# Spreading the modulation products of a two-block transformer kernel over its stages anew

## The chip, the cores and the metric

The kernel runs on one core of a Trainium2 chip. The core has four engines that compute (PE for matmuls, VectorE written DVE, ScalarE written ACT, GpSimd written POOL) and SyncE (SP), which here issues most of the transfers. The metric is the time of one execution on the device in microseconds, less is better; it is the median of three runs.

## The reference, cut to what matters

Two blocks are applied in turn to x, 256 tokens of 2048 features. The first block has two layers (differential attention, then forgetting attention with shared keys and values), the second has one layer (an S5 state-space mixer with a GLU, then an MLP). Every layer's shift, scale and gate come from a product of a conditioning vector with a large matrix; these are the modulation products.

```python
def first_block(x, c, w_mod, ...):
    c_act = jax.nn.silu(c)
    for l in range(2):
        shift, scale, gate = jnp.split(c_act @ w_mod[l] + b_mod[l], 3, axis=-1)   # 2048 x 6144
        h = x * (1.0 + scale[:, None]) + shift[:, None]
        if l == 0:
            y = diff_attention(h, a_w_in, a_w_out, ...)
        else:
            kshift, kscale = jnp.split(c_act @ kv_w_mod + kv_b_mod, 2, axis=-1)   # 2048 x 4096
            k, v, F = project(x * (1.0 + kscale[:, None]) + kshift[:, None], kv_w)
            y = forgetting_attention(h, b_w_in, b_w_out, k, v, F)
        x = layer_norm(DN_ALPHA * x + gate[:, None] * y, ln_g[l], ln_b[l])
    return x

def second_block(x, c, ctx, c_ctx, w_mod, ...):
    sh1, sc1, gt1, sh2, sc2, gt2 = adaln(c, w_mod)           # silu(c) @ w_mod + b: 2048 x 12288
    csh1, csc1, *_ = adaln(c_ctx, w_mod)
    h_lat = modulate(rmsnorm(x, norm_mix_pre), sh1, sc1)
    h_ctx = modulate(rmsnorm(ctx, norm_mix_pre), csh1, csc1)
    # a complex linear recurrence over the tokens in both directions, then gelu and GLU
    y = s5_mixer(h_ctx, h_lat, ...)
    x = x + gt1 * rmsnorm(y, norm_mix_post)
    h = modulate(rmsnorm(x, norm_mlp_pre), sh2, sc2)
    return x + gt2 * rmsnorm(jnp.square(jax.nn.relu(h @ w_mlp_in)) @ w_mlp_out, norm_mlp_post)
```

## The kernel before

All activations stay on the core; the weights pass through it once. They come in 320 items of 1 MB, each two tiles of 128 x 1024 numbers. For each tile SP loads it, ACT casts it to a coarser number wh (L130), VectorE forms the rest wl = w - wh (L131), and PE multiplies wh and wl with the activations, 48 matmuls for an item (L156 to L158, L193 to L195), 32 in the MLP (L169, L170). Items 0 to 63 are layer 0's in-projections, 64 to 79 its out-projection, 80 to 111 keys and values, 112 to 143 queries and gates of layer 1, 144 to 159 its out-projection. Then come the S5 norm and the recurrences, whose scans (L1405 to L1407) run on VectorE and POOL. Items 160 to 191 are the GLU, 192 to 319 the MLP.

A modulation product is written as steps (`gemv`). One segment of 2048 columns has two halves of 8 steps; a step loads 1 MB in two tiles graw from a pool of four buffers. It is computed on PE (L215: 8 matmuls that the profile shows as 16 records) or on VectorE (L230: two products that add to an accumulator gacc; the first of an accumulator is ACT's, L228). At the end of a half the accumulators are brought together on PE (L239), copied by ACT (L242), selected on PE (L245) and added to the bias by POOL (L250). There are 224 steps: m0 (layer 0), mk (keys and values), m1 (layer 1), mc = m2_0 and m2_1 with two vectors at once, which always run on PE, and m2_2 to m2_5 (the gate of the S5 layer, shift, scale and gate of the MLP).

The steps are strung on a list. With each item `bg()` asks a policy, a cycle of engine names set at the start of each stage (P_L0A, P_KV, ...), whether and on which engine the list's next step is to run beside that item. So the table of constants at the head of the kernel spreads the products over the stages, and `bg_finish()` runs what is missing of a segment just ahead of its use. In the same way `step()` advances side work (tables for S5, the context's states) by the amounts in P_CTX and the like. A step's arithmetic is issued one step later than its loads. After that a scheduler with a timeline of its own sets each engine's order when the program is built, so that instructions also move against the order of the code.

Of the kernel before, what the change touches and what calls it, by code (L numbers as in the profile page):

```python
# [47 lines left out]
SCANS = ((0,), (2,), (3, 4))  # L48
SLOT = (0, 0, 1, 0, 1)
P_START = ("pe",)  # L50
P_L0A = ('dve', 'pe')
P_KV = ('dve', 'pe')
P_QG = ('dve', 'dve', 'pe')
P_W = ("pe",)
P_GLU = ('dve',)
P_MLP = ('dve', None, None)
P_ON0 = ('dve', 'dve', 'dve', None)
P_ON1 = ('pe', 'dve', None)
BG_V = 5
BG_W = 0  # L60
PF_N = 6
ZT = 'm'
PF_POOL = 1
PF = 1
# [2 lines left out]
INC = ('pj', 'pj')  # L67
BG_K = 6
BG_Q = 0
P_CTX = (1,)  # L70
HL = 5
JOBS = ("m0", "m02", "mk", "m1", "mc", "m12", "m22", "m24", "m25")
DVE_W = 1
DVE_V = 1
POOL_V = tuple(range(7))
BG_M = 4
BG_B = 2
TL = True
KTS = 1
ENG = {'m0': 'dve', 'mc': 'pe', 'mk': 'dve', 'm1': 'dve', 'm2': 'pe'}  # L80
HOLD = 0
E_K = "x"
X_GLU = (0,)
X_KV = (0,)
X_L0A = (0,)
# [4 lines left out]
X_QG = (0,)  # L90
X_START = (0,)
X_W = (0,)
PV_ACT = 1
POL0 = ('dve', 'dve', 'dve', None)


def view(t, off, dims):
# [9 lines left out]
class K:  # L107
# [178 lines left out]
    def bg(self, n=1, eng=None):  # L286

        for _ in range(n):
            e = eng or next(self.pol)
            if e and self.bgq and not (self.hold and self.bgq[0][0].startswith("m2")):  # L290
                name, gen, left = self.bgq[0]
                use = gen.send(ENG[name[:2]] if e == "x" else e)
                self.late.append((name, use))
                self.bg_use(LATE)
                self.bgq[0] = (name, gen, left - 1)
                if left == 1:
                    self.bgq.pop(0)
# [584 lines left out]
    def layer0(self):  # L882
# [73 lines left out]
        self.side.append(gen)  # L956
        self.policy(P_L0A, X_L0A)
        prev = None
# [38 lines left out]
        self.ctx_rms()  # L997
        self.policy(P_ON0, X_ON0)
        self.norm = self.out_norm(o_, m0[2], 0)
# [109 lines left out]
    def layer1(self):  # L1109
# [52 lines left out]
        kT, v = [], []  # L1162
        self.policy(P_KV, X_KV)
        vgen = self.s5_outputs_table(self.act.tile([128, 4096], F32, name="gen2_ws", tag="act"))
        self.side.append(vgen)
        for j in range(32):
            if j == 1:
                F = forget()
            if j == 3:
                forget_t(F)  # L1170
            if j < 16:
                ps = self.mm_t(k_)
                t = self.kv.tile([128, T], F32, name=f"k{j}", tag="kv")
                with self.tc.issue_after(nc.scalar.copy(t, ps).ins):
                    nc.scalar.activation(z[:, j], z[:, j], AF.Identity, scale=V("lg0")[:, j:j + 1],
                                         bias=V("lb0")[:, j:j + 1])
                kT.append(t)
            else:
                ps = self.mm_n(k_, j % 2)
                if j % 2:  # L1180
                    for h in range(2):
                        t = self.kv.tile([128, 2, 128], F32, name=f"v{j - 17 + h}", tag="kv")
                        nc.scalar.copy(t, ps[:, :, h * 128:h * 128 + 128])
                        v.append(t)
# [54 lines left out]
        def start_ctx():  # L1239
            if self.ctx is None and not self.bg_open("mc_0") and not self.bg_open("mc_1"):  # L1240
                Sc, Bc = self.small_bg("sc", V("mixpre"), self.mc[1], None, self.mc[0])
                self.ctx = self.ctx_states(Sc, Bc)
                self.side.append(self.ctx)
                self.steps = itertools.cycle(P_CTX)

        self.ctx = None
        self.policy(P_QG, X_QG)
        for h in range(16):
# [88 lines left out]
    def s5_mix(self):  # L1337
# [173 lines left out]
        self.bg_finish("m2_2")  # L1511
        self.policy(P_GLU, X_GLU)
        gs = self.vt.tile([128, KT], F32, name="gs1")
# [215 lines left out]
```

## Time and profile before

| | us |
|---|---|
| median of 3 runs (2577.77 to 2581.68) | 2579.72 |
| the profiled execution | 2582.58 |
| its span, from the first to the last instruction | 2580.7 |
| PE busy in it | 2374.7 (92%) |
| VectorE busy | 1806.7 (70%) |
| ScalarE busy | 1255.4 (49%) |
| GpSimd busy | 211.5 (8%) |
| mean granted TensorE clock, as a share of full speed | 0.939 |

Busy times of different engines overlap. PE's matmuls are pipelined, so one that takes 0.28 us by its record can begin 0.12 us after the one before it; the spacing of the starts is what PE work costs. The stages follow one another on one time axis and can be told apart by the item whose first matmul begins there: layer 0 from 113 us, layer 1's keys and values from 698.6, queries from 964.5, its out-projection from 1240.8, GLU from 1572.8, MLP from 1829.3.

### The profile page before, as it was taken

What the parts mean: (1) busy time and instruction counts of PE and PEld (TensorE: products, weight loads), DVE (VectorE), ACT (ScalarE), POOL (GpSimd) and SP (SyncE); (2) the same over time, 40 slices, a digit from 0 to 9 for tenths busy, and PEclk for the clock granted to TensorE, in tenths of its full rate; (3) what the DMA queues carried; (4) which work ended last, traced back from release to release, by engine and by line L of the source; (5) the groups of instructions that cost most, each with busy time, mean ns of one, the idle gap of its engine ahead of it and who ended that gap; (6) DMA issues with size and microseconds to landing.
All of it is one profiled execution on the core that took longest, in us unless ns stands there. A gap on an engine that the chain in (4) does not pass through costs nothing.

```text
span 2580.7 us, 48360 instructions
## 1 busy us (share of the span) xinstructions
PE 2374.7 (92%) x18950; PEld 2054.5 (80%) x18950; DVE 1806.7 (70%) x3351; ACT 1255.4 (49%) x2178; POOL 211.5 (8%) x432
## 2 busy tenths in 40 slices
PE   5699999999899999999998634999799999999997
PEld 1299999999688888889986424999688888888885
DVE  3287778878775565788877999876765565665655
ACT  1455554454365555766654335544544443443442
POOL 0000000000011110000000754000000000000000
PEclk7599999999889999999998766999899999999998
DMA  9999999878869998888876634897366666666662
GB/s 322 343 341 324 326 323 339 311 259 321 263 237 337 325 334 296 281 269 272 276 237 213 208 108 138 320 316 263 113 188 190 190 190 186 186 187 191 190 185 93
DMA packets 203316, 644.66 MB, mean 250 GB/s; under 512 B 41008, under 2 KB 49456, under 8 KB 202704
## 3 DMA queue, kind: packets, MB, share of 16 engines
q1 hardware_dynamic: 195616, 620.47, 71.7%
q0 software_dynamic: 7472, 21.11, 2.1%
q8 instruction: 148, 2.42, 0.4%
q14 instruction: 80, 0.66, 0.1%
HBM read 613.71 MB, written 25.69 MB: 248 GB/s over the span
## 4 chain that ended last, share of the span: by engine, by line
PE 82%; DVE 11%; DMA 4%; ACT 2%; issue 1%; SPq 0%; DVEq 0%; POOL 0%; ACTq 0%
PE pj L169 18%; PE pj L156 12%; PE pj L157 12%; PE pj L158 12%; PE pj L170 9%; DMA graw<-in_w_mod 3%; PE g L215 3%; DVE scan_t L1406 3%; PE pjv L193 3%; PE pjv L194 2%; DVE scan_t L1405 2%; PE pjv L195 2%; DVE S L1407 2%; PE inc L690 1%; PE st L363 1%
## 5 line engine op out<-in xcount | busy, mean ns | idle before, releaser
L131 DVE TENSOR_TENSOR wl<-w,wh 128x1024 fp32r<-128x1024 f32 x638 | 778.4, 1224 | 471.8 <-ACT wh L130 462.3
L130 ACT CAST wh<-w 128x1024 fp32r<-128x1024 f32 x640 | 665.6, 1048 | 699.6 <-PE pj L169 280.6
L169 PE MATMUL pj<-h,wh 128*128 128x512 f32 x1024 | 363.3, 400 | 6.1 <-DVE h L413 4.3
L169 PE MATMUL pj<-d,wh 128*128 128x512 f32 x1024 | 358.6, 396 | 0.0
L170 PE MATMUL pj<-h,wl 128*128 128x256 f32 x1024 | 287.5, 281 | 1.1 <-DVE wl L131 1.1
L230 DVE SCALAR_TENSOR_TENSOR gacc<-graw,csilu,gacc 128x1024 f32<-128x1024 f32 x207 | 265.1, 1281 | 32.7 <-DMA graw<-in_w_mod 23.3
L170 PE MATMUL pj<-d,wl 128*128 128x256 f32 x1024 | 284.8, 279 | 0.0
L169 PEld LDWEIGHTS pj<-h,wh 128*128 128x128 f32 x1024 | 194.1, 190 | 54.6 <-issue 3.9
L169 PEld LDWEIGHTS pj<-d,wh 128*128 128x128 f32 x1024 | 191.9, 188 | 47.4 <-PE pj L170 1.7
L156 PE MATMUL pj<-hH,wh 128*128 128x256 f32 x768 | 221.4, 289 | 5.4 <-ACT hH L412 4.0
L158 PE MATMUL pj<-hH,wl 128*128 128x256 f32 x768 | 221.3, 289 | 0.5 <-DVE wl L131 0.5
L157 PE MATMUL pj<-hL,wh 128*128 128x256 f32 x768 | 221.0, 288 | 0.0
L215 PE MATMUL g<-graw,czc 128*32 128x256 f32 x1776 | 170.2, 467 | 53.0 <-DMA graw<-in_w_mod 50.0
L170 PEld LDWEIGHTS pj<-h,wl 128*128 128x128 f32 x1024 | 194.8, 190 | 1.5 <-DVE wl L131 1.5
L170 PEld LDWEIGHTS pj<-d,wl 128*128 128x128 f32 x1024 | 192.8, 188 | 0.4
L156 PEld LDWEIGHTS pj<-hH,wh 128*128 128x128 f32 x768 | 148.7, 194 | 9.0 <-ACT hH L412 4.1
L215 PEld LDWEIGHTS g<-graw,czc 128*32 128x32 f32 x1776 | 46.8, 119 | 132.7 <-DMA graw<-in_w_mod 107.9
L158 PEld LDWEIGHTS pj<-hH,wl 128*128 128x128 f32 x768 | 148.5, 194 | 4.5 <-issue 3.7
L157 PEld LDWEIGHTS pj<-hL,wh 128*128 128x128 f32 x768 | 148.7, 194 | 3.8 <-issue 3.7
L158 PE MATMUL pj<-z,wl 128*128 128x256 f32 x512 | 145.6, 285 | 2.9 <-POOL wl L131 2.7
L156 PE MATMUL pj<-z,wh 128*128 128x256 f32 x512 | 147.3, 289 | 1.0 <-ACT wh L130 1.0
L250 POOL TENSOR_TENSOR m<-gs,vecs 128x4 f32<-128x4 f32 x48 | 19.4, 428 | 1567.3 <-ACT gs L247 1567.3
(473 smaller groups left out, 5494.3 us busy)
## 6 DMA issues: line engine op xcount, KB each, us to landing
graw<-in_w_mod SPq DMA_DIRECT2D x384, 512.0 KB, 5.8
w<-in_mlp_in SPq DMA_DIRECT2D x128, 512.0 KB, 4.5
w<-in_mlp_out SPq DMA_DIRECT2D x128, 512.0 KB, 4.3
w<-in_a_in SPq DMA_DIRECT2D x96, 512.0 KB, 6.5
graw<-in_w_kvmod SPq DMA_DIRECT2D x64, 512.0 KB, 6.6
w<-in_b_in SPq DMA_DIRECT2D x64, 512.0 KB, 5.8
w<-in_glu SPq DMA_DIRECT2D x64, 512.0 KB, 5.4
w<-in_a_v SPq DMA_DIRECT2D x32, 512.0 KB, 5.6
```

Source lines behind the costliest of these rows:

```text
L130: nc.scalar.copy(h, src)
L131: (eng or (nc.gpsimd if next(self.spl) else nc.vector)).tensor_sub(l, src, h)
L156: self.nc.tensor.matmul(ps, h, aH, start=kt == order[0], stop=False)
L157: self.nc.tensor.matmul(ps, h, aL, start=False, stop=False)
L158: self.nc.tensor.matmul(ps, l, aH, start=False, stop=kt == order[-1])
L169: self.nc.tensor.matmul(ps, h, view(aH, 0, [[T, 2], [1, T]]), start=kt == order[0], stop=False)
L170: self.nc.tensor.matmul(ps[:, 0], l, aH, start=False, stop=kt == order[-1])
L193: self.nc.tensor.matmul(ps[:, i], aH[:, s], h, start=half == 0 and i == 0 and k == 0, stop=False)
L194: self.nc.tensor.matmul(ps[:, i], aH[:, s], l, start=False, stop=False)
L215: nc.tensor.matmul(st["g"][32 * q:32 * q + 32], self.cz[c][:, ch * 2 + s], raw[s][:, q * 256:q * 256 + 256], start=st["n"] == 0, stop=ch = ...
L230: nc.vector.scalar_tensor_tensor(acc, raw[s], cc, acc, op0=MUL, op1=ADD)
L1406: e.tensor_add(u, t[:, :, 0], s[:, :, :, c + 1])
```

## The change

Constants of the table are changed, and `bg()` takes a policy entry that is a tuple, for several steps beside one item. Beside layer 0 fewer steps are taken in the first half and one in three on PE in the second. HOLD = 1 keeps m2_2 to m2_5 waiting until the S5 mixer begins. While they are held, mc takes the places in the queries. BG_M = 16 steps are issued at the start of the recurrences, and three (BG_V) beside each of three scan groups. The GLU takes every fourth step on PE. The S5 output table (LATE_V) is put on the side work's list at item 3 of keys and values instead of ahead of them, and P_QG2 is a policy that applies from where the context's states begin.

```diff
-P_L0A = ('dve', 'pe')
-P_KV = ('dve', 'pe')
-P_QG = ('dve', 'dve', 'pe')
+P_L0A = ('pe', None, 'dve', None)
+P_KV = ('pe', None, 'dve', 'pe', None)
+P_QG = ('pe', ('pe', 'pe'))
+P_QG2 = ('dve', 'pe')
-P_GLU = ('dve',)
+P_GLU = ('dve', 'dve', 'dve', 'pe')
-P_ON0 = ('dve', 'dve', 'dve', None)
-P_ON1 = ('pe', 'dve', None)
-BG_V = 5
+P_ON0 = ('dve', 'pe')
+P_ON1 = (None,)
+BG_V = 3
+LATE_V = 3
-P_CTX = (1,)
+P_CTX = (1, 1, 2, 1)
-BG_M = 4
-BG_B = 2
+BG_M = 16
+BG_B = 3
-HOLD = 0
-E_K = "x"
+HOLD = 1
+E_K = "pe"
-POL0 = ('dve', 'dve', 'dve', None)
+POL0 = ('dve', 'dve', 'pe')
...
             e = eng or next(self.pol)
-            if e and self.bgq and not (self.hold and self.bgq[0][0].startswith("m2")):
+            for e in e if isinstance(e, tuple) else (e,):
+                if not e or not self.bgq or self.hold and self.bgq[0][0].startswith("m2"):
+                    continue
...
         vgen = self.s5_outputs_table(self.act.tile([128, 4096], F32, name="gen2_ws", tag="act"))
-        self.side.append(vgen)
         for j in range(32):
+            if j == LATE_V:
+                self.side.append(vgen)
...
                 self.steps = itertools.cycle(P_CTX)
+                self.policy(P_QG2, X_QG)
```

The changed file's lines are two to six further on than those of before. Three places show how instructions stand now.

VectorE between layers 0 and 1, where the layer norm (L1103, L1104; after L1107, L1108) and the low part kL of the key input (L413; after L417) are made. L547, L548, L628 and L630 (after L551, L552, L632, L634) are table work. Before:

```order
792 L1104 TENSOR_TENSOR xres<-xres,lnb 128x256
793 L1103 TENSOR_TENSOR xres<-xres,lnb 128x256
794 L413 TENSOR_TENSOR kL<-u,kH 128x256
795 L628 TENSOR_TENSOR gen_ws<-vprod 128x32x16
796 L230 SCALAR_TENSOR_TENSOR gacc<-graw,csilu,gacc 128x1024
797 L1104 TENSOR_TENSOR xres<-xres,lnb 128x256
798 L1103 TENSOR_TENSOR xres<-xres,lnb 128x256
799 L413 TENSOR_TENSOR kL<-u,kH 128x256
800 L547 TENSOR_TENSOR vprod<-gen_ws 128x512
801 L548 TENSOR_TENSOR vprod<-gen_ws 128x512
802 L230 SCALAR_TENSOR_TENSOR gacc<-graw,csilu,gacc 128x1024
```

The same place of VectorE's order after the change:

```order
754 L417 TENSOR_TENSOR kL<-u,kH 128x256
755 L1108 TENSOR_TENSOR xres<-xres,lnb 128x256
756 L1107 TENSOR_TENSOR xres<-xres,lnb 128x256
757 L417 TENSOR_TENSOR kL<-u,kH 128x256
758 L632 TENSOR_TENSOR gen_ws<-vprod 128x32x16
759 L1108 TENSOR_TENSOR xres<-xres,lnb 128x256
760 L1107 TENSOR_TENSOR xres<-xres,lnb 128x256
761 L417 TENSOR_TENSOR kL<-u,kH 128x256
762 L551 TENSOR_TENSOR vprod<-gen_ws 128x512
763 L552 TENSOR_TENSOR vprod<-gen_ws 128x512
764 L1108 TENSOR_TENSOR xres<-xres,lnb 128x256
```

The products (L230) are gone from between the norm's rows; the table work stands there as before.

VectorE where the GLU's output is added to the residual (L1567, L1568, L1580; after L1573, L1574, L1586) and the MLP's input h is made (L413; after L417). L327 (after L331) is the end of the reciprocal square root ahead of it. Before:

```order
2571 L327 SCALAR_TENSOR_TENSOR ry<-rq,ry 128x2
2572 L1562 COPY rr<-ry 128x2
2573 L1567 SCALAR_TENSOR_TENSOR U<-U,gs_18613,rrb 128x256
2574 L1568 TENSOR_TENSOR xres<-xres,U 128x256
2575 L1580 TENSOR_TENSOR xn<-xres,rrb 128x256
2576 L1567 SCALAR_TENSOR_TENSOR U<-U,gs_18613,rrb 128x256
2577 L1568 TENSOR_TENSOR xres<-xres,U 128x256
```

After:

```order
2494 L232 SCALAR_TENSOR_TENSOR gacc<-graw,csilu,gacc 128x1024
2495 L331 SCALAR_TENSOR_TENSOR ry<-rq,ry 128x2
2496 L1568 COPY rr<-ry 128x2
2497 L232 SCALAR_TENSOR_TENSOR gacc<-graw,csilu,gacc 128x1024
2498 L1573 SCALAR_TENSOR_TENSOR U<-U,gs_18660,rrb 128x256
2499 L232 SCALAR_TENSOR_TENSOR gacc<-graw,csilu,gacc 128x1024
2500 L1574 TENSOR_TENSOR xres<-xres,U 128x256
2501 L232 SCALAR_TENSOR_TENSOR gacc<-graw,csilu,gacc 128x1024
2502 L1586 TENSOR_TENSOR xn<-xres,rrb 128x256
2503 L1573 SCALAR_TENSOR_TENSOR U<-U,gs_18660,rrb 128x256
2504 L232 SCALAR_TENSOR_TENSOR gacc<-graw,csilu,gacc 128x1024
```

Products of m2_5 stand here among rows between which there was none.

VectorE's product gs of the gate m2_2 with the vector of the post-norm (L1514; after L1520). Before it stands beside layer 1's out-projection, among the context's rows (L1328 to L1331):

```order
1478 L230 SCALAR_TENSOR_TENSOR gacc<-graw,csilu,gacc 128x1024
1479 L1330 TENSOR_TENSOR ctx_ws<-ctx_ws 128x512
1480 L1053 TENSOR_TENSOR xres<-xres,kb_14435 128x256 x9
1481 L1514 SCALAR_TENSOR_TENSOR gs_18613<-m_2_110,vecs 128x16
1482 L131 TENSOR_TENSOR wl_1_15264<-w_1_15261,wh_1_15263 128x1024
```

After:

```order
2052 L1411 TENSOR_TENSOR scan_t<-S_15954,scan_t 128x64
2053 L1412 TENSOR_TENSOR scan_t<-scan_t,S_15955 128x32
2054 L1520 SCALAR_TENSOR_TENSOR gs_18660<-m_2_110,vecs 128x16
2055 L1412 TENSOR_TENSOR scan_t<-scan_t,S_15954 128x32
2056 L1413 TENSOR_TENSOR S_15955<-scan_t 128x32
```

It has moved in between the scans of the recurrences.

## Rows read from the trace of the kernel before

**Rows 1.** Windows by stage: length, then each engine's busy time, clock, DMA

```profile
core 0: us, PE busy (x) PEld busy (x) DVE busy (x) ACT busy (x) POOL busy (x), PEclk, DMA share, GB/s
113.00:363.00 250.00, 244.94 (x2086) 225.44 (x2087) 197.95 (x307) 128.28 (x232) 17.86 (x38) 0.98 0.94 333
363.00:570.00 207.00, 207.00 (x1738) 204.23 (x1737) 164.96 (x242) 99.16 (x164) 3.69 (x8) 1.00 0.88 312
570.00:683.00 113.00, 113.00 (x890) 99.97 (x890) 87.29 (x121) 52.34 (x83) 4.18 (x4) 1.00 0.85 297
683.00:735.00 52.00, 38.71 (x196) 31.39 (x196) 44.61 (x92) 25.62 (x51) 3.02 (x11) 0.67 0.68 216
735.00:964.00 229.00, 229.00 (x2402) 199.24 (x2404) 134.34 (x188) 127.89 (x244) 38.83 (x86) 1.00 0.92 321
964.00:1241.00 277.00, 276.26 (x2412) 243.58 (x2405) 206.28 (x363) 183.63 (x380) 10.24 (x18) 1.00 0.83 282
1241.00:1373.00 132.00, 130.95 (x1166) 113.62 (x1168) 101.52 (x182) 65.44 (x119) 4.51 (x10) 1.00 0.78 256
1413.00:1607.00 194.00, 98.89 (x1480) 75.76 (x1479) 188.80 (x757) 83.81 (x150) 113.35 (x224) 0.71 0.49 158
1607.00:1813.00 206.00, 204.05 (x1699) 189.29 (x1700) 151.47 (x152) 107.10 (x169) 9.60 (x10) 0.99 0.83 288
1813.00:1861.00 48.00, 34.77 (x159) 27.39 (x157) 37.53 (x100) 25.19 (x45) 0.00 (x0) 0.79 0.22 69
```

**Rows 2.** Modulation products on PE: the page's group, then windows of L215 alone

```profile
L215 PE MATMUL g<-graw,czc 128*32 128x256 f32 x1776 | 170.2, 467 | 53.0 <-DMA graw<-in_w_mod 50.0
...
113.00:363.00 250.00, 21.52 (x272) 5.45 (x272) 0.98 0.94 333
735.00:964.00 229.00, 33.34 (x458) 13.17 (x461) 1.00 0.92 321
1413.00:1607.00 194.00, 22.55 (x224) 6.09 (x224) 0.71 0.49 158
```

**Rows 3.** Timeline of PE, keys and values, then layer 0: start, us

```profile
809.65 0.28 PE L158 MATMUL pj<-kH,wl 128*128 128x256 f32 x1
809.86 1.07 PE L215 MATMUL g<-graw,czc 128*32 128x256 f32 x16
...
811.08 0.28 PE L157 MATMUL pj<-kL,wh 128*128 128x256 f32 x1
...
250.82 0.28 PE L157 MATMUL pj<-hL,wh 128*128 128x256 f32 x1
251.03 0.64 PE L215 MATMUL g<-graw,czc 128*32 128x256 f32 x8
...
251.82 0.28 PE L156 MATMUL pj<-hH,wh 128*128 128x256 f32 x1
```

**Rows 4.** Timeline of VectorE between layers 0 and 1

```profile
691.83 1.28 DVE L230 SCALAR_TENSOR_TENSOR gacc<-graw,csilu,gacc 128x1024 f32<-128x1024 f32 x1
...
697.80 1.28 DVE L230 SCALAR_TENSOR_TENSOR gacc<-graw,csilu,gacc 128x1024 f32<-128x1024 f32 x1
699.00 0.41 DVE L1104 TENSOR_TENSOR xres<-xres,lnb 128x256 f32<-128x256 f32 x1
...
704.49 0.68 DVE L547 TENSOR_TENSOR vprod<-gen_ws 128x512 f32<-128x512 f32 x1
```

**Rows 5.** Windows, the norm between layers 0 and 1 (columns of rows 1)

```profile
697.00:731.00 34.00, 25.57 (x119) 22.94 (x120) 33.93 (x68) 18.97 (x37) 1.64 (x3) 0.63 0.67 211
```

**Rows 6.** Timeline of VectorE from GLU to MLP, with waits in brackets

```profile
1819.92 0.16 DVE L378 TENSOR_SCALAR var<-ysum 128x2 f32<-128x2 f32 x1 [2.53 <-PE ysum L373]
...
1825.79 0.48 DVE L1567 SCALAR_TENSOR_TENSOR U<-U,gs,rrb 128x256 f32<-128x256 f32 x1 [1.31 <-PE rrb L336]
```

**Rows 7.** Timeline of PE at the end of the recurrences

```profile
1608.71 3.68 PE L1464 MATMUL y<-vl,sn 128*64 128x64 f32 x64 [6.34 <-ACT sn L1458]
...
1620.04 0.71 PE L1495 MATMUL zt<-idn,zb 64*128 64x64 f32 x12
```

**Rows 8.** Windows, POOL alone, the last stretch of the recurrences

```profile
1560.00:1607.00 47.00, 15.66 (x17) 0.68 0.32 103
```

## Prediction

> **What bounds the kernel now.** I read the table of windows first, one row for each stage of the program [rows 1]. The figures to compare are PE's busy time with the stage's length. From 113 to 683 us, from 735 to 1373 and from 1613 to 1813 PE is busy for 98 to 100% of the time at a granted clock of 0.98 to 1.00 (2.4 GHz): 244.94 of 250 us beside layer 0's first half, 207.00 of 207, 229.00 of 229 beside keys and values. VectorE has 20 to 40% to spare there. So in these stages a product on PE lengthens the kernel and a product on VectorE costs nothing. In four short stages it is the other way round. Between layers 0 and 1 (683 to 735) PE has 38.71 of 52 us, at a clock of 0.67; in the 34 us of it from 697 on VectorE is busy for 33.93 [rows 5]. From 1813 to 1861 PE has 34.77 of 48, and around the S5 recurrences (1413 to 1607) VectorE has 188.80 of 194 while PE has 98.89 at a clock of 0.71. There it is VectorE's work that lengthens the kernel, and PE work is free as long as it doesn't stand ahead of what the chain needs.
>
> **Price of a step.** A step is one megabyte of a modulation matrix. On PE it is 16 records of L215. In the timeline beside keys and values one matmul begins at 809.65, the 16 records follow, and the second matmul after them begins at 811.08: 1.43 us, of which two ordinary spacings of 0.12 are not the step's. That is 1.19 us a step [rows 3]. Where a step is cut in two eights it is (251.82 - 250.82) - 0.24 = 0.76 each, 1.52 a step; layer 0's first half has it so. On VectorE a step is two products, each 1.20 us from its start to the next one's, 697.80 to 699.00 [rows 4]. Before, 111 steps are on PE (1776 records of L215, [rows 2]) and 113 on VectorE; as built after the change 144 and 80.
>
> **The PE-bound stages.** The steps on PE, counted in the two built programs: layer 0's first half 16 before, 8 after; its second half 0 and 10; its out-projection 0 and 8; keys and values 29, and after the change 16 with 6 more that were on VectorE ahead of them and now stand among their first items; queries and gates 14 and 31; layer 1's out-projection 6 and 0; GLU 0 and 8. For the first and the fourth [rows 2] shows the records before (272 and 458, 16 to a step, with a neighbour's step among the 272). Costs: -8 x 1.52 = -12.2; +10 x 1.19 = +11.9; +8 x 1.19 = +9.5; -7 x 1.19 = -8.3; +17 x 1.19 = +20.2; -6 x 1.19 = -7.1; +8 x 1.19 = +9.5. Sum **+23.5 us**. In all these stages PE has no idle time worth naming that could take the 22 net steps. Bounds: every added step cut in eights makes it 30 x 1.52 - 12.2 = 33; each at the 1.07 us that its 16 records are busy [rows 3] makes it 20. The VectorE steps that go away there gain nothing, since VectorE waited there anyway.
>
> One rule speaks for a larger gain in layer 0. The transfers there keep the DMA engines 0.94 busy at 333 GB/s [rows 1], and the first half loses 16 of its 32 steps, 16.8 MB, which is 50 us at that rate. The Trainium skill, "DMA: Bandwidth & Descriptors", Specifications, gives about 358 GB/s as what the memory yields to one core; by it this stage would be close to that limit, and the 50 us would be worth something. The trace speaks against it: PE's idle time in the stage is 250 - 244.94 = 5.1 us, so nothing beyond these 5.1 us can come from lighter transfers. The second half takes 8 steps more, 8.4 MB on 207 us at 312 GB/s: 73 MB in 219 us, which is 333 GB/s again, the rate that the first half bears beside a full PE.
>
> **Between layers 0 and 1.** The DVE order of the changed program has no product in the norm's chain any more. Before, seven, the first at 697.80, stand among the rows that make the key input (L1103, L1104, L413), on an engine without a gap, and two more ahead of them in the chain of the sums, the second at 691.83. 9 x 1.20 = **-10.8 us**. The table work of the S5 outputs (12 rows of about 0.6, one in [rows 4]) is not moved out of this stretch by its later start: in the new order the same twelve rows stand between the same norm rows, 7.2 us. So the "table work later" brings nothing here. PE's own work from 697 to 731 is 25.57 us at a clock of 0.63, so at that clock this part can shrink by 34 - 25.57 = 8.4 us, which is the seven products' time; with the clock at 1.00 it could shrink by up to 20. I take -10.8, with 0 (PE follows at the low clock and catches nothing) and -20 as ends.
>
> **Into the recurrences.** Three VectorE products go away from the layer norm and the context work ahead of the scans, between 1371 and 1382. One of them waited for its transfer in idle time; two lie in the chain: **-2.4 us**, between -4 and 0.
>
> **During the recurrences.** 25 steps stand on PE there instead of 14, beside PE's 95 us of idle time: 11 x 1.19, twice that at half the clock, are hidden. Their transfers add 11.5 MB to 158 GB/s x 194 us = 31 MB: hidden too. VectorE's scans set the length and have the same rows as before. At the end PE's order changes: before, 56 GLU matmuls stand between the last y (its 64 records begin at 1608.71) and the transposes zt at 1620.04 [rows 7]; after, 25. If zt is ready no sooner, PE waits 31 x 0.12 = **+3.7 us**; between 0 (zt was ready long before) and 5.2 (12 matmuls fewer also fill the 6.34 us of waiting ahead of y).
>
> **From GLU to the MLP.** The steps of the S5 layer and MLP that were held back don't end in the GLU any more. The last seven (m2_5) come from the MLP's items in program order, but the scheduler puts 12 of their products on VectorE into this stage, in which there was none before: one ahead of the last xy, one behind it, three inside the rsqrt chain, one ahead of the first residual row and six between the first residual rows. Two fall into waits that last at least as long (2.53 us before the chain at 1819.92, 1.31 before L1567 at 1825.79, [rows 6]). Ten are on the path: 10 x 1.20 = **+12.0 us**. Bounds: 0 if all are swallowed by waits (PE has 13 us idle here, 48 - 34.77, but VectorE is gapless from 1825.79 on, so I don't think so), +18 if the products also wait for their transfers, of which only four buffers (two steps) can be ahead.
>
> **Sum.** 23.5 - 10.8 - 2.4 + 3.7 + 12.0 = +26.0 us. The profiled execution took 2582.58 us with a span of 2580.7; it would be 2608.6. It lies 2.9 us above the median of the runs shown, so the forecast for the median is 2579.72 + 26, rounded to **2605 us**.
>
> **The rivals.** (a) *The chain between the layers was worth more, and the GLU's end is free.* VectorE without products lets PE run at full clock: -20 there. Layer 0 gives its 5.1 idle us back, the start of the recurrences -4, PE steps cost their low end of 20, and the products towards the MLP vanish in waits: 20 - 20 - 5 - 4 = -9, 2571 us. For it: PE's clock of 0.63 in just that stretch. Against it: the added PE steps are in stages with no gap at all. It decides if the stretch from 697 to 731 shrinks by more than 15 us. Chance 0.13. (b) *About the same:* the low end of 20 with -15 between the layers, -2.4 into the recurrences, and 0 to +2 where recurrences and GLU end gives +2.6 to +4.6, 2582 to 2584. Chance 0.12 for within 0.2% (5.2 us, about what a measurement of this kernel can tell from no change). (c) *The recurrences stall.* In the new DVE order the product of the gate m2_2 with its vector stands inside the last scan group, after 486 of 756 scan rows, where before it stood ahead of them, beside layer 1's out-projection. It waits for POOL's last add of m2_2, which stands after 169 of 189 POOL scan rows, and for PE's steps of m2_2 with their transfers. At an even pace VectorE reaches that row at 1413 + 486 / 756 x 194 = 1538, and POOL, which has only 17 of its 224 instructions of the stage left at 1560 [rows 8], is past its 169th scan row by then or a little before: the two points lie close together. If it comes 10 to 15 us late, the scans behind it are late as much, since VectorE has 5 us to spare in 194 [rows 1]: 2615 to 2620. Chance 0.10. (d) *The change doesn't do what it says:* the held steps would be run by the finishing calls on PE instead of by VectorE. The built counts show 144 and 80, so I give it no chance of its own; the part on the table work has this fate.
>
> **How the numbers follow.** The forecast has 0.65, (a) 0.13, (b) 0.12, (c) 0.10. With the ends of the single terms the forecast alone spans 2588 to 2622. To leave out no more than 2 in 10 the range goes from 2578, which takes in (b) and leaves out most of (a), to 2626 past (c). Faster 0.13, same 0.12, slower 0.75.
>
> **What would show it.** In the profile after: L215's line with 2304 records instead of 1776 and the products' on VectorE some 60 fewer; queries and gates (964 to 1241, 277 us in [rows 1]) longer by 16 to 20 us and layer 0's first half shorter by some 12; the stretch from layer 0's last matmul to the key projection shorter by about 11 with the table rows still in it; the way from the last GLU matmul to the MLP longer by about 12, with products between the residual rows. I'm wrong if PE steps in the queries cost clearly less than 1 us, if the stretch between the layers shrinks by over 15, or if the MLP starts without delay.

## The result and the profile after

The changed kernel takes **2623.8 us** (median of four, 2620.39 to 2629.21) against 2580.32 (also of four) for the kernel before: a ratio of 1.0172, interval 1.0152 to 1.0191. The forecast was 2605, range 2578 to 2626, slower. So sign and range held, and the size fell short: +43.5 us by the medians against +26. The profiled execution (2620.39 us, span 2618.6) is the fastest of the four; against the one of before it is 37.8 us longer. The other 5.7 us are the place of the two profiled executions among their kind (2.3 above the one median, 3.4 below the other), so no stage shows them.

Windows of the changed kernel by stage (length, then busy time of PE, PEld, DVE, ACT, POOL, PE's clock, DMA share, GB/s):

```profile
111.00:350.00 239.00, 233.92 (x1961) 222.60 (x1961) 184.70 (x294) 131.41 (x233) 19.03 (x36) 0.97 0.87 302
350.00:570.00 220.00, 218.41 (x1895) 208.60 (x1887) 156.95 (x234) 97.47 (x161) 4.26 (x8) 1.00 0.89 306
683.00:735.00 52.00, 44.02 (x335) 35.41 (x336) 37.30 (x87) 28.35 (x59) 3.49 (x13) 0.90 0.49 164
735.00:952.00 217.00, 212.81 (x2192) 189.32 (x2189) 129.31 (x179) 124.00 (x234) 37.36 (x77) 1.00 0.90 309
952.00:1108.00 156.00, 152.71 (x1335) 122.17 (x1339) 68.21 (x119) 76.11 (x155) 6.62 (x21) 0.98 0.83 285
1108.00:1259.00 151.00, 143.34 (x1322) 128.40 (x1311) 116.72 (x215) 102.15 (x212) 2.50 (x3) 0.99 0.78 264
1831.00:1898.00 67.00, 44.02 (x234) 33.39 (x226) 53.66 (x115) 28.43 (x51) 0.48 (x2) 0.77 0.48 159
```

Beside [rows 1], PE now has 3.3 and 7.7 us without work in the two halves of the queries and 4.2 in keys and values, where before it had 0.7 in all queries and none in keys and values. The modulation products' group in the page, as in [rows 2], shows the built 144 steps of 16 records:

```profile
L217 PE MATMUL g<-graw,czc 128*32 128x256 f32 x2304 | 211.8, 457 | 59.0 <-DMA graw<-in_w_mod 57.2
```

For a balance I cut both traces at the first matmul of the item that opens each stage. Each entry is a difference of such starts, so the column of changes adds up to the difference of the profiles. Single entries are less certain: the start, whose steps no experiment below touches, takes 111.1 to 115.8 us in the profiles of the change and its variants.

```
stage (items)                  before   after   change   forecast
start, to item 0                113.1   111.1    -2.0       0
layer 0, first half (0)         249.8   239.0   -10.8     -12.2
layer 0, second half (32)       206.9   220.0   +13.2     +11.9
layer 0, out-projection (64)    106.6   112.7    +6.0      +9.5
between the layers (79)          73.5    62.5   -11.0     -10.8
keys and values (84)            214.7   207.0    -7.7      -8.3
queries, first half (112)       139.7   156.1   +16.3   } +20.2
queries, second half (128)      136.6   150.4   +13.7   }
layer 1, out-projection (144)   124.8   120.6    -4.2      -7.1
S5 and recurrences (159, 160)   248.5   251.2    +2.7      +1.3
GLU (161)                       194.0   200.9    +6.9      +9.5
GLU to MLP (191)                 53.0    66.9   +13.9     +12.0
MLP to the end (196)            719.5   720.3    +0.8       0
```

All terms but one are within 3.5 us; the queries cost 30.1 instead of 20.2. One near hit hides two errors that cancel, as the end of the recurrences will show.

**The queries.** I counted PE's time there by the spacing of starts, taking what a spacing has over 0.45 us as waiting. The steps went from 18.0 us (224 records) to 36.5 (512), +18.5: close to the forecast's 20.2 for 17 steps, though by this count it is 18 steps at 1.03 each. Waiting went from 0.5 to 9.8, and the 1536 projection matmuls from 191.5 to 197.9, +6.4. Work of the context's states that falls into these items is 6.1 less (inc, 320 records to 256). PE's waits in the first half and in the second half of the queries (us in total, times, longest; groups over 1 us; none is for a product's own transfer):

```profile
PE pj L159 <- DVE h1L L417: 2.9, 1, 2.9
...
PE inc L694 <- DMA wc<-d_w: 3.6, 3, 1.4
PE tp L1228 <- ACT ws L1223: 3.6, 1, 3.6
```

The first is read further in VectorE's timeline. It is the start of the first query item, which takes 11.7 us from its first matmul to the next item's:

```profile
950.82 0.69 DVE L551 TENSOR_TENSOR vprod<-gen_ws 128x512 f32<-128x512 f32 x1 [3.61 <-DMA gen_ws<-in_s5c]
...
953.59 0.68 DVE L552 TENSOR_TENSOR vprod<-gen_ws 128x512 f32<-128x512 f32 x1
954.19 1.22 DVE L133 TENSOR_TENSOR wl<-w,wh 128x1024 fp32r<-128x1024 f32 x1
955.32 0.42 DVE L417 TENSOR_TENSOR h1L<-u,h1H 128x256 fp32r<-128x256 f32 x1
955.66 0.68 DVE L634 TENSOR_TENSOR gen_ws<-vprod 128x512 f32<-128x512 f32 x1
```

The table work that was put on the list later (LATE_V) is not done when the keys and values end. What is left is run just ahead of the queries, on the engine that must make the low part h1L of their input. So the move brought little between the layers (e1, which undoes it, takes 3.0 us longer there) and a wait where I had not looked.

The wait costs more than its own length. PE's granted clock was 1.00 from 940 to 952 us and fell behind it, to 0.50, the lower of its two levels (1.2 GHz), from 956 to 960. Windows of the changed kernel:

```profile
952.00:958.00 6.00, 2.71 (x12) 2.50 (x13) 5.93 (x13) 5.95 (x16) 0.58 (x1) 0.61 0.29 79
958.00:964.00 6.00, 6.00 (x54) 5.70 (x54) 2.97 (x8) 3.89 (x12) 0.26 (x1) 0.82 0.61 198
```

The projection matmuls of this one item take 8.4 us by their spacing instead of 5.9, which is 2.5 of the 6.4 us above. In e1, without the wait, the clock is 1.00 from 950 to 980 us, across the start of the queries at 956.2, and these matmuls take 6.8.

**Between the layers.** VectorE's timeline; the norm's rows with the table work among them and no product, as the built order had it:

```profile
703.01 0.42 DVE L417 TENSOR_TENSOR kL<-u,kH 128x256 fp32r<-128x256 f32 x1
...
704.00 0.69 DVE L551 TENSOR_TENSOR vprod<-gen_ws 128x512 f32<-128x512 f32 x1
704.61 0.68 DVE L552 TENSOR_TENSOR vprod<-gen_ws 128x512 f32<-128x512 f32 x1
705.21 0.42 DVE L417 TENSOR_TENSOR kL<-u,kH 128x256 fp32r<-128x256 f32 x1
```

Nine products at 1.20 us [rows 4] were to save 10.8 us; it is 11.0.

**GLU to MLP.** The same engine, between the residual rows, where no product stood before the change:

```profile
1852.98 1.28 DVE L232 SCALAR_TENSOR_TENSOR gacc<-graw,csilu,gacc 128x1024 f32<-128x1024 f32 x1 [1.49 <-DMA graw<-in_w_mod]
...
1855.85 0.48 DVE L1573 SCALAR_TENSOR_TENSOR U<-U,gs,rrb 128x256 f32<-128x256 f32 x1
1856.73 1.28 DVE L232 SCALAR_TENSOR_TENSOR gacc<-graw,csilu,gacc 128x1024 f32<-128x1024 f32 x1 [0.39 <-DMA graw<-in_w_mod]
1857.93 0.42 DVE L1574 TENSOR_TENSOR xres<-xres,U 128x256 f32<-128x256 f32 x1
1858.26 1.28 DVE L232 SCALAR_TENSOR_TENSOR gacc<-graw,csilu,gacc 128x1024 f32<-128x1024 f32 x1
```

Ten products were priced at 12.0 us; the stage grew by 13.9, and the two waits for transfers in these rows are 1.88.

**The end of the recurrences.** The scans themselves did not stall: from VectorE's last copy of the increments into the state S (L1388 at 1412.6 before, L1394 at 1420.4 after) to its last scan row they take 194.8 us before and 193.2 after. The way from layer 1's last item to that copy became 5.8 us shorter (forecast 2.4). But the way from the end of the last scan row to the first matmul of item 161 grew from 6.6 to 16.7 us. Three engines' timelines of the changed kernel tell why:

```profile
1596.11 1.14 ACT L1487 ACTIVATE y<-y 128x512 f32<-128x512 f32 x2
1613.82 1.05 ACT L1464 COPY sn<-S 64x1024 f32<-64x1024 f32 x1 [16.58 <-DVE S L1413]
1614.78 0.63 ACT L1493 ACTIVATE y<-y 128x512 f32<-128x512 f32 x1
1615.43 0.63 ACT L1487 ACTIVATE y<-y 128x512 f32<-128x512 f32 x1
...
1616.20 1.26 POOL L1490 TENSOR_TENSOR zb<-y,zb 128x512 f32<-128x512 f32 x1 [16.84 <-ACT y L1487]
...
1617.52 0.77 PE L1501 MATMUL zt<-idn,zb 64*128 64x64 f32 x8 [15.08 <-POOL zb L1490]
1618.22 1.97 PE L1439 MATMUL y<-ml,U 128*64 128x64 f32 x32
1619.98 3.93 PE L1470 MATMUL y<-vl,sn 128*64 128x64 f32 x90
1626.47 1.15 PE L1470 MATMUL y<-vl,sn 128*64 128x64 f32 x32 [2.57 <-DVE wl L133]
```

ScalarE's copy sn of the last block waits for the last scan, and behind it in ScalarE's order stand two activations (L1493, then L1487) of an earlier block. POOL's zb waits for the second, PE's transposes zt wait for zb, and behind them on PE stand the last two blocks' matmuls y. Most of these need nothing of the last scan: the 32 of L1439, and 58 of L1470 that belong to the last block but one, whose copies sn were through at 1594.4 (its first six ran at 1601.81). In the kernel before, the same two activations (there L1487 and L1481) ran ahead of the copy:

```profile
1591.83 0.63 ACT L1487 ACTIVATE y<-y 128x512 f32<-128x512 f32 x1 [0.86 <-POOL y L1484]
1592.49 0.63 ACT L1481 ACTIVATE y<-y 128x512 f32<-128x512 f32 x1
...
1607.62 1.99 ACT L1458 COPY sn<-S 64x1024 f32<-64x1024 f32 x2 [9.87 <-DVE S L1407]
```

and zt was through at 1597, before the scans ended at 1607.6; only 64 matmuls y were left. There the last y begins 4.5 us after the last scan, here 13.6.

### The profile page after: what moved, and what is told of

Same layout as the page of the kernel before. It is cut to its first block, busy times and chain, and to the rows that moved or that the text cites. A ratio compares the mean times of both kernels' runs of the same rounds, so it can differ in the third digit from the quotient of the medians.

```text
span 2618.6 us, 49285 instructions
## 1 busy us (share of the span) xinstructions
PE 2399.5 (92%) x19462; PEld 2057.0 (79%) x19462; DVE 1732.2 (66%) x3287; ACT 1257.7 (48%) x2176; POOL 208.6 (8%) x432
## 5 line engine op out<-in xcount | busy, mean ns | idle before, releaser
L171 PE MATMUL pj<-h,wh 128*128 128x512 f32 x1024 | 363.4, 400 | 11.7 <-DVE h L417 8.6
L217 PE MATMUL g<-graw,czc 128*32 128x256 f32 x2304 | 211.8, 457 | 59.0 <-DMA graw<-in_w_mod 57.2
L171 PEld LDWEIGHTS pj<-h,wh 128*128 128x128 f32 x1024 | 194.1, 190 | 60.9 <-DVE h L417 10.8
L232 DVE SCALAR_TENSOR_TENSOR gacc<-graw,csilu,gacc 128x1024 f32<-128x1024 f32 x143 | 183.3, 1282 | 85.8 <-DMA graw<-in_w_kvmod 42.0
L172 PEld LDWEIGHTS pj<-h,wl 128*128 128x128 f32 x1024 | 194.8, 190 | 1.8 <-DVE wl L133 1.6
L217 PEld LDWEIGHTS g<-graw,czc 128*32 128x32 f32 x2304 | 58.5, 118 | 152.6 <-DMA graw<-in_w_mod 119.3
L158 PE MATMUL pj<-h1H,wh 128*128 128x256 f32 x512 | 149.1, 293 | 1.0 <-ACT h1H L416 0.6
L159 PE MATMUL pj<-h1L,wh 128*128 128x256 f32 x512 | 147.3, 289 | 2.9 <-DVE h1L L417 2.9
```

The source lines that it names most:

```text
L158: self.nc.tensor.matmul(ps, h, aH, start=kt == order[0], stop=False)
L159: self.nc.tensor.matmul(ps, h, aL, start=False, stop=False)
L171: self.nc.tensor.matmul(ps, h, view(aH, 0, [[T, 2], [1, T]]), start=kt == order[0], stop=False)
L172: self.nc.tensor.matmul(ps[:, 0], l, aH, start=False, stop=kt == order[-1])
L217: nc.tensor.matmul(st["g"][32 * q:32 * q + 32], self.cz[c][:, ch * 2 + s], raw[s][:, q * 256:q * 256 + 256], start=st["n"] == 0, stop=ch = ...
L232: nc.vector.scalar_tensor_tensor(acc, raw[s], cc, acc, op0=MUL, op1=ADD)
```

## The experiments

They are named as their records are (e1 to e13; there is no e7). All of them compute the whole result. "Behind" a row means that the scheduler may not place an instruction ahead of it; nothing else of the instruction changes. Stage times are cut as in the table above, from each kernel's profile.

**e1: the table work where it was.**

```
-LATE_V = 3
+LATE_V = 0
```

> The changed kernel with one constant undone: the S5 output table goes on the side work's list ahead of keys and values again (LATE_V = 0 instead of 3). The steps stand on the same engines. Theory: with the late start the table's last rows stand on VectorE and ScalarE among the rows that make the queries' input, the first query item took 11.7 us instead of 6.5, and this is part of the 10 us by which the queries grew beyond the price of their steps. Then the first query item falls to 6.5 to 8 us and the kernel gains 4 to 6 us, to about 2618. Rival: the queries are longer only by their products on PE; then nothing changes, 2624 within 3.

2619.24 us, ratio to before 1.0155 (1.0139 to 1.0172), 4.6 less than the changed kernel, as expected. The first half of the queries fell from 156.1 to 145.5, and PE's wait for h1L is gone; but the first item still takes 9.6 us, not 6.5 to 8. One and a half steps, 2.1 us by spacing, stand earlier in this kernel, so some 8.5 of the 10.6 us were the table's. Half came back: between the layers it takes 65.5 us instead of 62.5, and the second half of the queries grew from 150.4 to 156.0, with other waits:

```profile
PE pj L158 <- ACT ctx_ws L1320: 6.2, 3, 3.6
PE inc L694 <- DMA wc<-d_w: 3.7, 3, 2.3
```

Both belong to the context's states, the next work on the side list.

**e2: the MLP's products behind the MLP's tenth item.**

```
-P_MLP = ('dve', None, None)
+P_MLP = (None,) * 10 + ('dve', None, None) * 39
...
+                with self.tc.issue_after(self.gate):
+                    use()
```

> The changed kernel with the last seven steps of m2_5 run on VectorE behind the MLP's tenth item, and held there in VectorE's order, instead of on the way from GLU to MLP; nothing else moves. Theory: ten to twelve of their products lay on the way at 1.20 us each, 191's to 196's first matmul grew by 14.0 us. They leave, and the MLP hides them: 12 to 14 us faster, about 2611, with that way back at 53 us. Rival: the way is longer because of the weights' transfers, which the steps' transfers delay, or because of the clock that PE has there, so that the products were only in the way of nothing: under 4 us gained, 2620 or more.

2613.31 us, 1.0130 (1.0113 to 1.0147). GLU to MLP took 53.1 instead of 66.9, -13.8, as expected and as before the change. The products are the whole cause there. The MLP, where they run now, grew by 2.6, so it doesn't hide them entirely; by the medians the gain is 10.5.

**e3: layer 1's lead steps on VectorE, as before the change.**

```
-E_K = "pe"
+E_K = "x"
```

> The changed kernel with one constant undone: the six steps at the start of layer 1 run on VectorE again (E_K). 96 PE records go, eleven products come back on VectorE between layers 0 and 1, three of them between the norm's rows. Theory: PE gives 6 x 1.19 = 7 us back beside the first key items, VectorE's chain between the layers takes 3.6 to 9 us more: -3 to +2 in sum, 2621 to 2626, with the way from 79's to 84's first matmul longer by 4 to 9. Rival: the chain between the layers was not what PE waited for, the gain of 11 us there came from elsewhere: the way stays at 62 us and the kernel is 7 us faster.

2639.31 us, 1.0230 (1.0215 to 1.0245), 13 us above the end of what was expected. Between the layers 75.2 instead of 62.5: +12.7, where I had put 3.6 to 9. Thirteen products stand there, none in the changed kernel. Eleven of them stand from the row behind the norm's sums on, and 11 at 1.20 are 13.2. The gain I expected in keys and values did not come: 206.6 against 207.0. The records of L217 between 683 and 735 in the changed kernel say why:

```profile
683.00:735.00 52.00, 4.01 (x56) 1.74 (x56) 0.90 0.49 164
```

56 records are three and a half steps, in a stretch in which PE has 8 us without work. Counted by items, four of the six lead steps stand between the layers and two beside the keys and values. So there was next to nothing to give back: that part of my expectation was wrong. The price of a product in the chain held, and my count of those in it was too low.

**e4: layer 0's second half and out-projection without steps on PE.**

```
-P_ON0 = ('dve', 'pe')
+P_ON0 = ('dve',)
-POL0 = ('dve', 'dve', 'pe')
+POL0 = ('dve',)
```

> The changed kernel with all 48 steps beside layer 0's second half and out-projection on VectorE, instead of 30 there and 18 on PE. No product comes between the norm's rows by it. Theory: these two stages are PE's, and 18 steps x 1.19 us are 21 us: 2602, VectorE hides its 36 more products (206 us busy of 320). Rival: the transfers, at 306 GB/s, or VectorE set the pace there: under 8 us gained, 2616 or more, with PE waiting for wl.

2603.76 us, 1.0091 (1.0076 to 1.0106), -20.0. The two stages lost 14.4 and 8.6 us for 18 steps, 1.28 each against the forecast's 1.19. This is the price of a step on PE beside full PE, measured by itself. Against my expectation some of the products moved on: six of them stand between the layers now, which take 66.8 us instead of 62.5.

**e5: as e1, and the context's work one step per item.**

```
-LATE_V = 3
+LATE_V = 0
-P_CTX = (1, 1, 2, 1)
+P_CTX = (1,)
```

> The kernel e1_table_early with a second constant undone: the side work for the context's states advances by one piece per item again (P_CTX = (1,)) and not by 1, 1, 2, 1. Theory: in the queries' second half PE waits 3.6 us for the context's weights wc and 3.6 us for ScalarE's copy of the attention weights, which stands behind side work, and before the change it waited for neither; with even pieces these waits go: 4 to 7 us less from 128's to 144's first matmul, 2612 to 2615. Rival: the pieces run anyway and only move into layer 1's out-projection, or the waits come from the products' transfers: within 2 us of e1, 2617 to 2621.

2617.05 us, 1.0143 (1.0124 to 1.0163), in the rival's range. The queries' second half fell from 156.0 to 135.8 and PE has no wait left in the queries; 9.6 us of that were its waits there, and 5.5 are work of the context (inc) that left the stage. But the S5 stage grew from 252.1 to 270.4: the context's work now ends after layer 1 and holds the scans up, of which VectorE's first row begins 60 us after item 159's first matmul (8 in e1). The cost moved and did not go.

**e6: all beside layer 0, keys and values and GLU on VectorE, with e1 and e2.**

```
-P_L0A = ('pe', None, 'dve', None)
-P_KV = ('pe', None, 'dve', 'pe', None)
+P_L0A = ('dve', None)
+P_KV = ('dve', None, 'dve', 'dve', None)
-P_QG2 = ('dve', 'pe')
-P_GLU = ('dve', 'dve', 'dve', 'pe')
+P_QG2 = ('dve',)
+P_GLU = ('dve',)
+ ... and the edits of e1, e2 and e4
```

> The changed kernel with every step that need not be on PE moved to VectorE where PE is busy (layer 0 from the first item, keys and values, the queries' second half, GLU), the table early as in e1, and m2_5's last steps in the MLP as in e2. PE keeps the startup, mc's 32 steps, the six between layers 0 and 1, two in the queries and the 25 beside the recurrences. Theory: the terms add up, since each stage waits for PE alone: -4.6 (e1), -10.5 (e2), -20.0 (e4), 8 steps x 1.52 = -12.2 in layer 0's first half, 7 x 1.19 = -8.3 beside keys and values, 6 x 1.19 = -7.1 in the queries, -6.9 in GLU: 69.6 us less, 2554, faster than the kernel before by 1%. Rival: with 96 more products VectorE, or the transfers at over 300 GB/s, become what layer 0 and GLU wait for; then the gain stops at what e1, e2 and e4 gave, 2585 to 2590.

2584.08 us, 1.0014 (1.0005 to 1.0024), 30 above what was expected and close to the rival's 2585, though the loss is not where the rival put it. The stages themselves did as priced: against the changed kernel layer 0 lost 33.1 us in three stages, keys and values 8.3, GLU 5.2, GLU to MLP 13.1. But between the layers it took 3.8 more, with the six products of e4, and the queries' second half grew by 18.3, to 168.7; PE's longest waits in the queries:

```profile
PE tp L1234 <- ACT ws L1229: 7.0, 3, 4.0
PE pj L158 <- ACT ctx_ws L1326: 6.9, 2, 3.6
PE inc L699 <- DVE ws L1271: 5.9, 2, 4.7
```

**e8: as e6, the table work behind the norm's last row.**

```
+                with self.tc.issue_after(self.vgate):
+                    done = next(self.side[0], True)
...
+        self.vgate = self.nlast
```

> The kernel e6_all_dve with the S5 output table's work held on VectorE behind the layer norm between layers 0 and 1, in order only, without a wait. Theory: that stretch is VectorE's; the twelve table rows of 0.60 us between its rows lengthen it by 7.2 us, as six products did by 1.20 each in e3, and the late start of the table in the change missed them. 7 us faster than e6, with the way from 79's to 84's first matmul shorter by as much; some of it may come back where the table now ends, ahead of the queries. Rival: PE at its low clock is what the stretch waits for, or the table's rows come back in full ahead of the queries: within 2 us of e6.

2580.34 us, 0.9999 (0.9990 to 1.0009). 3.7 faster than e6, half of what was expected. Between the layers -2.0 instead of -7, keys and values -2.4, the queries -1.5 and +1.8, GLU -1.9 in the profiles.

**e9: the changed kernel with mc done during keys and values.** The context's states need mc; after the change mc is done eight items later (128 instead of 120).

```
-P_KV = ('pe', None, 'dve', 'pe', None)
+P_KV = ('pe', 'dve', 'pe') * 3 + ('pe',) * 23
```

> The changed kernel with a step beside every item of keys and values (32 instead of 19), so that mc, which the context's states wait for, is done by item 118 and they start at item 120, as before the change, and not at 128. The 13 steps are mc's, on PE in either place; the queries have 13 fewer. Theory (new, from e5 and e6): the late end of mc delays the context's chain, which must end before the recurrences; squeezed into 32 items it makes PE wait in the queries' second half, or at the recurrences. Then keys and values grow by 13 x 1.19 = 15.5 us, the queries shrink by that and by some 8 to 10 us of waits: 2613 to 2617. Rival: the queries' waits are the products' own bursts on PE and their transfers; then only the 15.5 us move, and 13 more transfers beside keys and values cost something: 2622 to 2630.

2634.55 us, 1.0212 (1.0196 to 1.0227), some 18 above what was expected and above the rival's 2630 too. Keys and values grew by 9.8. The second half of the queries fell by 14.5 and layer 1's out-projection by 10.2, but the first half took 178.2, 22.1 more, one item of it 32.7. My theory that the late mc is the cause falls. The item of 32.7 us is 121, beside the first of the context's states, so the waits moved with these. The longest in the queries:

```profile
PE pj L158 <- ACT ws L1257: 7.1, 1, 7.1
PE inc L694 <- DMA wc<-d_w: 4.4, 3, 2.1
PE g L217 <- DMA graw<-in_w_mod: 4.2, 3, 2.4
```

**e10 and e11: as e8, mc early; then also the context even.**

```
+P_KV = ('dve',)
+P_QG = ('dve', ('dve', 'dve'))
+P_CTX = (1,)          # e11 only
```

> The kernel e8_table_behind with a step beside every item of keys and values, so that the context's states start at item 120 instead of 132. In e6 and e8 the gains of layer 0, GLU and the two norms (some 60 us by the stages) were given back from item 128 to the end of the recurrences, which took 500 and 504 us against 469 before the change. Theory: that is the context's chain started late; 30 us of it go: 2545 to 2555, 1 to 1.3% faster than before the change. Rival: the chain isn't what is late there, or VectorE, with 33 more products than before the change ahead of the recurrences, is: 2570 or more.

> The kernel e10_dve_mc_early with the context's side work in even pieces (P_CTX = (1,)), as before the change. Theory: from item 120 on even pieces end in time for the recurrences, and they spare PE the waits that the doubled pieces make; within 4 us of e10, rather faster. Rival, by e5, where even pieces from item 128 on made the recurrences end 18 us later: they end late here too, and this kernel is over 8 us slower than e10.

2588.66 us, 1.0041 (1.0029 to 1.0052), and 2582.74, 1.0012 (1.0003 to 1.0021). The rival of e10 came, over 30 us above what I expected. The first half of the queries took 182.6 and 182.3. Two items stand out. Item 115 took 20 us in both, 8.9 in the changed kernel; at its end, at 969.0 in both, stands the table's last large store (d_v), 47 us into the queries, where in the changed kernel it is 4. The other is item 121, 31 and 28 us, beside the context's first states. ScalarE's timeline in e11 shows it, and PE's the wait:

```profile
1030.48 0.38 ACT L1272 ACTIVATE ws<-pj 128x256 f32<-128x256 f32 x1 [0.67 <-PE sc L1225]
...
1034.02 3.13 ACT L1327 ACTIVATE ub<-uctx,ctx_ws 64x64 f32<-64x64 f32 x7
...
1037.66 4.04 ACT L1327 ACTIVATE ub<-uctx,ctx_ws 64x64 f32<-64x64 f32 x9
1041.73 0.80 ACT L1238 ACTIVATE ws<-ws,sr 128x128 f32<-128x128 f32 x2
...
1042.19 1.09 PE L1243 MATMUL tp<-idn,ws 128*128 128x128 f32 x3 [8.77 <-ACT ws L1238]
```

Sixteen small activations of the context, seven and nine, run ahead of the two (L1238) that the attention of this item needs. As at the recurrences' end, it is ScalarE's order that holds PE up, here behind rows that are busy and not behind one that waits.

**e12: as e11, one step per item in the queries, the table two steps and one by turns, the context slow at first.**

```
+P_QG = ('dve',)
+P_CTX = (1,) * 20 + (1, 2) * 8
+        self.steps = itertools.cycle((2, 1))
```

> The kernel e11_dve_mc_even with three things evened out: one step beside each of the queries' first items instead of two steps beside every other; the table's work by two pieces beside every other item of keys and values, so that in VectorE's order it ends ahead of the queries' input; the context in even pieces from item 124 to the end of the queries, then by one and a half an item. The steps stand on the same engines. Theory (after e9 to e11): the queries' excess, 22 us of PE's waits in e9 and e11 and 10 in the change, is from these bursts: transfers at 400 GB/s, the table's rows between the queries' rows, ScalarE's context rows ahead of the softmax copies. With evened pieces the first half of the queries takes 140 to 150 us instead of 182 and the kernel 2540 to 2560. Rival: these stages are full, the work only moves on to the next one, as from e1 to e5: 2575 or more, with the loss in the queries' second half or at the recurrences.

2576.22 us, 0.9989 (0.9978 to 1.0000), the fastest median, not to be told from the kernel before. The queries' first half took 138.4 and the second 142.6, but keys and values 235.6. The last item of these alone took 48.7; in the 51 us around it PE is without work for 20.5, at a clock of 0.78. Windows of e12:

```profile
900.00:951.00 51.00, 30.51 (x372) 18.41 (x371) 20.24 (x38) 22.39 (x55) 13.49 (x30) 0.78 0.84 293
735.00:900.00 165.00, 163.41 (x1625) 149.21 (x1624) 113.96 (x144) 91.46 (x169) 26.70 (x53) 1.00 0.91 320
```

PE's waits in the first of these windows:

```profile
PE g L217 <- DMA graw<-in_w_mod: 11.2, 11, 3.0
PE kps L658 <- DMA gen_ws<-d_b: 6.2, 1, 6.2
```

**e13: as e12, without the row that holds the table back.**

```
-        self.vgate = self.nlast
```

> The kernel e12_even_mc without the hold of the table behind the norm, so that the table's twelve first rows stand between the norm's rows again and its first store comes some 15 us sooner; nothing else is changed. Theory (from e6, e8 and e12): the S5 output table is a chain of its own, 231 to 247 us from its first store to its last in these kernels and in both kernels given, and the queries' input stands behind it; in e12 the last key and value item took 48.7 us for it. Started 15 us sooner it ends 15 us sooner, the norm gives up to 2 to 7 us of that back: 2563 to 2569, faster than before the change by 0.4 to 0.6%. Rival: the 48.7 us are the products' bursts and their transfers (PE waited 11 us for graw in them), which stay: 2576 to 2582.

2583.5 us, 1.0010 (1.0000 to 1.0020), just above the rival's range. Between the layers it took 6.4 us more, and the last item of keys and values still 41.9. That the table is a chain of fixed length which only starts too late falls: it started 12 us earlier (its first store at 687.2 instead of 699.2) and ended 3 us later (933.1 against 929.8). Both run their last rounds in a heap at the end. Why they are placed there stays open.

## Why the forecast came out as it did

- **The bound.** Stage by stage the reading held. A step cost 1.19 us beside a full PE by [rows 3]; 18 steps alone measured 1.28 (e4). A product in VectorE's chains cost 1.20 by [rows 4]; 11 of them measured 1.15 (e3).
- **Lighter transfers in layer 0.** The forecast weighed the rate of the transfers against PE's idle time of 5.1 us. The rate fell from 333 to 302 GB/s, and PE's time without work stayed 239 - 233.92 = 5.1. The gain is the steps' alone. The Trainium skill, "DMA: Bandwidth & Descriptors", Specifications, puts about 358 GB/s as the limit of one core; e11 has a stretch of 22 us at 400 (below), and the measurement decides. By the Trainium skill, the same page, Bandwidth, a core whose neighbour is idle gets more. The 400 agrees with that; no run here loads a second core.
- **The step that failed: "In all these stages PE has no idle time worth naming".** True of the kernel before, but the sum took it for the kernel after as well. The term +17 x 1.19 = +20.2 came out as +30.1: the steps at 18.5, and beside them 9.3 us of new waiting and 6.4 of slower matmuls, in part at the low clock behind a wait, less 6.1 of context work that left the stage and with some 2 of smaller parts. I followed the table work only to the norm ("brings nothing here"), not to the point where what is left of it must end, just ahead of the queries. e1 shows that some 8.5 us of the first half hang on that. In the second half the faster policy P_CTX makes the context's rows hold PE up; without it, in e5, that half is 20.2 us shorter, and the S5 stage 18.3 longer.
- **Into the recurrences and their end: right sum, wrong parts.** -2.4 was about -5.8: in the last 47 us of that way before, four products, 5.1 us, stood on VectorE; none does after. The end, taken as +3.7 from PE's order alone, was +10.1, because ScalarE's order had changed as well and I had not read it. With 1.6 us less in the scans that is the table's +2.7; that it lies near the forecast's +1.3 is luck. This is read from the timelines; no experiment varied it. All twelve have it: there the last y begins 13.4 to 16.1 us after the last scan. In e6, e8 and e10 to e13, which have one step on PE beside the GLU, the way from the last scan to the GLU's item 191 still takes 211.6 to 215.2 us against 200.6 before. One step costs 1.2 of these 11 to 15 us, so 9 us or more in each of them lie there. With ScalarE's activation ahead of the copy, e12 would be at an estimated 2576 - 9 = 2567; that was not tried.
- **GLU to MLP** was +13.9 for +12.0, close to the two transfer waits, 1.88 us, that I had put only into the upper bound.
- **The rivals.** (a) fails: the clock between the layers rose from 0.67 to 0.90, and the stretch still gained the nine products and no more (the forecast's figures for its upper end of 20 give 34 - 25.57 x 0.63 = 17.9). (b) fails with it. (c) fails in the place it named, since the scans lost nothing to the gate; a stall of its kind and size, though, was there at the end of them. (d) holds for the table work only, as said.
- **The range.** 2623.8 lies just beyond the 2588 to 2622 that the forecast alone was given, and inside 2578 to 2626 only by the room left for (c), which did not happen where it was named. That the range held is in part luck. The low ends of the terms add up to 2576 and the high ends to 2636; how 2588 to 2622 came of them the prediction doesn't say.

What stays open: how much of the waiting in the queries could be removed at all. Table and context run on ScalarE, VectorE and PE across four stages, and from e5 on part of what one of these stages lost came back in another. No run here separates the engines' share in that from the order in which the scheduler placed the work.

## What to carry to other kernels

Price a move stage by stage, by the engine that has no gap there; such prices held here to a few us. Then follow what the moved work stood in front of: side work that must be finished by a certain point ends up ahead of the next stage's input, and one small instruction behind a waiting one can hold three engines. Read the order of every engine at the joints, those that are mostly idle too, and don't add up gains of neighbouring stages that share such side work.

## What the runs showed of the hardware

A single core's transfers can go well above the rates of the stages in [rows 1]. A window of e11, at the fourth item of the queries, where the table ends; its GB/s hold the table's stores too:

```profile
948.00:970.00 22.00, 15.06 (x166) 10.54 (x166) 13.47 (x19) 7.41 (x15) 3.14 (x6) 0.87 1.03 400
```

And one of e9, beside a PE busy for 97%:

```profile
963.00:988.00 25.00, 24.33 (x240) 19.40 (x237) 16.83 (x31) 17.55 (x37) 3.69 (x8) 1.00 0.97 361
```

And ScalarE takes 0.45 us for each activation of 64 x 64 numbers (3.13 us for seven, L1327 of e11), where one of 128 x 256 (L1272) takes 0.38 in the same timeline, so sixteen of the former are 7 us in front of whatever stands behind them.
